# Tree attention on one core: more heads' slots laid side by side by GpSimd, and the first stores cut differently

## The chip, the core and the metric

The kernel runs on one core of one Trainium2 chip. The metric is the device time of one execution in microseconds (us). Three runs of the kernel before gave 133.4, 133.46 and 134.01 us; the median is 133.46 us.

## The reference

Batch 8 times 12 heads are 96 heads of 512 rows and 64 columns. Row `i` may look at itself and at its ancestors in a binary tree, nothing else.

```python
mask[i, i] = 1
parent = i
while parent > 0:
    parent = (parent - 1) // 2
    mask[i, parent] = 1
scores = np.einsum('bhqd,bhkd->bhqk', Q, K) * scale
scores = scores + (1 - mask) * (-1e9)
weights = np.exp(scores - np.max(scores, axis=-1, keepdims=True))
weights = weights / (np.sum(weights, axis=-1, keepdims=True) + 1e-10)
return np.einsum('bhqk,bhkd->bhqd', weights, V).astype(np.float32)
```

## The kernel before

The 96 heads are handled in 48 steps of two heads. The code of a step is written out in a fixed order (`FIRST`, then `SVK` and `SVQ` in turn), and each engine runs its own instructions in that order:

- **S**, scores: TensorE multiplies mask codes (L511, L544) and keys with queries (L519, L554) into PSUM, ScalarE takes the exponential into tiles `e` (L529, L560).
- **V**, values: TensorE multiplies the exponentials with the values `vt` into `ob` (L605); VectorE takes the reciprocal (L651) and writes the product to the output tile `of` (L653).
- **K** and **Q**, turning: from step 8 on, one K turn or one Q turn stands in every step and serves four heads, a few steps before their scores. TensorE transposes K or Q into `ktp` or `qtp`, VectorE copies them into `kq` (L470, L474, L478 for K; L493 for Q).

Heads are loaded in batches of eight (`KB`), so batch 3 is heads 24 to 31. Loads cast from float32 to bf16. In a batch as it is loaded, the two heads that a transpose needs side by side do not lie side by side, and a turn takes 16 transposes that fill 64 output partitions each (L450). For the batches in `LAID`, GpSimd first copies the batch into the tile `besideK` or `besideQ` (function `lay`, L433, two copies, one for each group of four heads), and a turn then takes 8 transposes of 128 output partitions (L441). There is one tile `besideK` and one `besideQ`, so `lay` of a batch also waits until the transposes of the batch before have read it.

The values of 16 heads (an octet of steps, numbered 0 to 5) are loaded into `vst` and spread into the tiles `vt` by GpSimd, VectorE and ScalarE (function `spread`, L364).

GpSimd's work is a list, `pool_program`: loads (`load_k`, `load_q`, `load_rows`, `load_leaves`), spreads, lays and stores (L662) in a fixed order. `ready` decides after which step an entry is written out, never its place in the list. GpSimd runs the list strictly in order; an entry that waits holds back all behind it. Every transfer but the first few and the last goes through this list, and each issue is an instruction of GpSimd. The last four heads are stored by SyncE.

Of the kernel before, what the change touches and what calls it, by code (L numbers as in the profile page):

```python
# [119 lines left out]
def kernel(  # L120
# [7 lines left out]
    nc = tc.nc  # L128
    B, H, S, D = Q.shape
    P = nc.NUM_PARTITIONS  # L130
# [5 lines left out]
    WIDE = 8  # L136
    KB, VB, VO = 8, 16, 16
    EIGHT = 2
    LAID = (8, 9, 10, 11)
    assert NH % VB == 0  # L140

    fp32 = mybir.dt.float32
# [126 lines left out]
    def head(i, a):  # L269

        return 2 * i + a if i < WIDE else 4 * (i // 2) + i % 2 + 2 * a
# [151 lines left out]
    def slots(st, i):  # L423
        return st[2 * i // KB].rearrange("p (g x) t d -> p g (x t) d", x=2)
# [167 lines left out]
    def values(i):  # L592

        if i < NP - 1:
            obs[i] = ob = psO.tile([P, 2, 512], fp32, name="ob")
        else:
            obs[i] = ob = psS.tile([P, 2, 512], fp32, name="s1")
        e1, e2, vt = ets[i], e2s[i % NE], vts[(head(i, 0) // VB) % NV]

        vtile = VTILE if i < WIDE else WVTILE  # L600
        parts = EIGHT_PARTS if head(i, 0) >= VB * EIGHT else PARTS[i >= WIDE]
        assert all(("vt", n, head(i, a)) in issued for n in parts for a in range(2))

        def product(e, a, t, tile_v, lo=0, hi=128, **flags):
            nc.tensor.matmul(  # L605
                out=ob[lo:hi, a, 65 * t:65 * t + 65],
                lhsT=e[:, a, PLACE[t], lo:hi],
                rhs=vt[vtile[tile_v][0]][:, head(i, a) % VB, vtile[tile_v][1], 0:D + 1],
                **flags,
            )  # L610

        def firsts(a):
            for t in range(4):
                product(e1, a, t, 0, start=t == 0, stop=False)

        def halves(a, last=True):
            for t in (0, 1):
                product(e2, a, t, 1 + SELF[t], 0, 64, start=False, stop=last and t == 1)
                product(e2, a, t, 1 + t, 64, 128, start=False, stop=last and t == 1)

        def wholes(a, last=False):
            for t in (2, 3):
                product(e2, a, t, 1 + t, start=False, stop=last and t == 3)

        if i == NP - 1:
            for a in range(2):
                firsts(a)
                wholes(a)
                halves(a)
        elif i >= 4 * LAID[0] - 4:  # L630
            for a in range(2):
                firsts(a)
            for a in range(2):
                halves(a, False)
# [25 lines left out]
    def store(eng, h0, n, step=1, p0=0, p1=P):  # L660
        g, f = divmod(h0, VO)
        return eng.dma_start(  # L662
            out=Or[p0:p1, h0:h0 + step * (n - 1) + 1:step, :],
            in_=ofs[g][p0:p1, f:f + step * (n - 1) + 1:step, :, :].rearrange(
                "p h t d -> p h (t d)"
            ),
        )

    DEALT = (0, 85, 87, 121, P)

    def store_rows(j0, j1):

        for j in range(j0, j1):
            store(nc.gpsimd, 0, 4, 1, DEALT[j], DEALT[j + 1])

    def pool_program():

        ops = [
            (load_k, 2, 2), (load_q, 2, 2), (load_v, 0, 4), (load_v, 4, 4),
            (load_k, 4, 4), (load_q, 4, 4), (load_k, 8, 4),  # L680
            (load_q, 8, 4), (load_v, 8, 8), (load_k, 12, 4),
            (load_q, 12, 4), (load_k, 16, 8), (load_q, 16, 4), (load_rows, 1, "upper"),
            (load_rows, 1, "even"), (load_rows, 1, "odd"), (load_q, 20, 4),
            (load_k, 24, 8), (load_q, 24, 8), (load_rows, 2, "upper"),
            (load_k, 32, 8), (load_leaves, 2, 0), (load_leaves, 2, 1),
            (load_q, 32, 8), (load_rows, 3, "upper"),
            (spread_pool, (1, "Z0", 8, 16), (1, "Z1", 8, 16)),
            (load_k, 40, 8), (load_q, 40, 8), (load_leaves, 3, 0), (load_leaves, 3, 1),
            (spread_top, 2, 0, 16), (spread_pool, (2, "Z0", 0, 16), (2, "Z1", 0, 16)),
            (load_q, 48, 8), (spread_pool, (2, "X", 0, 16)),  # L690
            (load_k, 48, 8), (spread_pool, (2, "N", 0, 16)),
            (load_rows, 4, "upper"), (spread_top, 3, 0, 16),
            (load_k, 56, 8), (load_q, 56, 8), (load_leaves, 4, 0), (load_leaves, 4, 1),
            (spread_pool, (3, "X", 0, 16), (3, "N", 0, 16), (3, "Z0", 0, 16), (3, "Z1", 0, 16)),
            (load_k, 64, 8), (store_rows, 0, 2), (load_q, 64, 8), (store_rows, 2, 4),
            (load_k, 72, 8), (spread_top, 4), (store, nc.gpsimd, 4, 12), (lay, "kst", 8),
            (load_q, 72, 8), (spread_pool, (4, "X", 0, 16), (4, "N", 0, 16)),
            (lay, "qst", 8), (load_rows, 5, "upper"),
            (spread_pool, (4, "Z0", 0, 16), (4, "Z1", 0, 16)),
            (load_leaves, 5, 0), (load_leaves, 5, 1), (load_k, 80, 8), (load_q, 80, 8),  # L700
            (store, nc.gpsimd, 16, 8), (lay, "kst", 9), (load_k, 88, 8), (load_q, 88, 8),
            (lay, "qst", 9), (store, nc.gpsimd, 24, 8), (store, nc.gpsimd, 32, 16),
            (spread_top, 5), (lay, "kst", 10), (store, nc.gpsimd, 48, 16), (lay, "qst", 10),
            (spread_pool, (5, "X", 0, 16), (5, "N", 0, 16)),
            (spread_pool, (5, "Z0", 0, 16), (5, "Z1", 0, 16)),
            (lay, "kst", 11), (store, nc.gpsimd, 64, 8), (lay, "qst", 11),
            (store, nc.gpsimd, 72, 8), (spread_leaves, 5, 1),
            (store, nc.gpsimd, 80, 8), (store, nc.gpsimd, 88, 4),
        ]
        return ops  # L710

    def ready(op, i):

        f, args = op[0], op[1:]
        if f in (load_k, load_q):
            return 2 * (i + 3) >= args[0] + args[1] - 4 * KB
        if f is load_v:
            return True
        if f in (load_rows, load_leaves):
            return 2 * i >= VB * (args[0] - 2)  # L720
        if f is spread_pool:
            tops = [(("vt", "M", VB * o + h) in issued) for o, part, h0, h1 in args if part == "X"
                    and o < EIGHT for h in range(h0, h1)]
            return 2 * i >= VB * (args[0][0] + 1 - NV) and all(tops)
        if f is store_rows:
            return 2 * i >= 4
        if f in (spread_top, spread_leaves):
            return 2 * i >= VB * (args[0] + 1 - NV)
        if f is lay:
            return turned[args[0]] >= 4 * args[1]  # L730
        return 2 * i >= -(-(args[1] + args[2]) // 4) * 4
# [15 lines left out]
    for o in range(EIGHT, NH // VB):  # L747
        for j in range(8):
            h0 = VB // 2 * (j // 4)
# [107 lines left out]
```

## Time and profile before

| what | value |
|---|---|
| median of three runs | 133.46 us |
| the profiled execution | 133.8 us |
| its span, first to last instruction | 131.9 us |
| TensorE matmul busy | 114.7 us (87%) |
| VectorE busy | 108.8 us (82%) |
| ScalarE busy | 94.4 us (72%) |
| GpSimd busy | 87.1 us (66%), 118 instructions |
| granted TensorE clock, mean | 0.978 |

In the profile PE is TensorE, PEld its weight loads, DVE is VectorE, ACT is ScalarE, POOL is GpSimd and SP is SyncE. The page gives a row of digits for each engine: the span in 40 slices of 3.3 us, each digit the busy share of a slice in tenths. A row of the timeline has the start and the length in us, the engine, the line, the operation, out<-in with the shapes, the count, and in brackets the idle time before it with what ended it. A row of the groups has after the first bar the busy time in us and the mean length of one in ns, and after the second bar the idle time before them. The profile counts issuing a transfer as busy time of POOL.

### The profile page before, as it was taken

How to read it: one execution, taken by the hardware profiler on the slowest of the kernel's cores; microseconds unless marked ns; L12 is line 12 of the kernel's file. 1: busy time of each engine (PE TensorE's matmuls, PEld its weight loads, DVE VectorE, ACT ScalarE, POOL GpSimd, SP SyncE). 2: the span in 40 equal slices, each digit the busy share in tenths (PEclk: the TensorE clock that was granted, in tenths of full speed). 3: DMA queues.
4: the chain of work that ended last, by engine and by line, in shares of the span. 5: the costliest groups of instructions: out<-in, count | busy, mean ns of one | idle time of the engine just before them, and what ended most of it. 6: DMA issues, size and time to landing. Idle time of an engine off the chain costs nothing.

```text
span 131.9 us, 5281 instructions
## 1 busy us (share of the span) xinstructions
PE 114.7 (87%) x2286; PEld 80.4 (61%) x2289; DVE 108.8 (82%) x261; ACT 94.4 (72%) x153; POOL 87.1 (66%) x118
## 2 busy tenths in 40 slices
PE   6883999999789699899899999999988999999920
PEld 2351576676566476666577677677765766776610
DVE  3438569988999989989999999999999999877350
ACT  4358268989768957968858787787868668688900
POOL 6994624245623998799951899999999977802200
PEclk9999599999999999999999999999999999999996
DMA  3999999999999999999999999999999999999984
GB/s 122 216 190 196 198 199 205 199 199 207 206 200 205 204 202 208 209 202 205 202 208 204 244 236 305 338 204 207 203 288 285 228 391 406 400 402 402 397 315 148
DMA packets 29719, 32.28 MB, mean 245 GB/s; under 512 B 1488, under 2 KB 26704, under 8 KB 29696
## 3 DMA queue, kind: packets, MB, share of 16 engines
q0 software_dynamic: 28416, 30.68, 115.2%
q1 hardware_dynamic: 864, 0.93, 2.1%
q10 hardware_dynamic: 416, 0.33, 1.0%
q8 instruction: 18, 0.29, 0.8%
q14 instruction: 5, 0.04, 0.1%
HBM read 37.96 MB, written 12.58 MB: 383 GB/s over the span
## 4 chain that ended last, share of the span: by engine, by line
DVE 38%; PE 24%; DMA 14%; POOL 10%; issue 5%; ACT 3%; ACTq 1%; POOLq 0%
DVE of L653 12%; DVE vt L364 11%; DMA kst<-in_K_dram 8%; PE ob L605 8%; DMA qst<-in_Q_dram 6%; POOL vt L364 5%; DVE rec L651 3%; PE s L511 3%; DVE kq L493 3%; DVE kq L470 3%; DVE kq L478 3%; DVE kq L474 3%; PE s L519 2%; ACT e L560 2%; PE s L544 1%
## 5 line engine op out<-in xcount | busy, mean ns | idle before, releaser
L529 ACT ACTIVATE e<-s 128x1024 bf16<-128x1024 f32 x40 | 40.9, 1023 | 20.7 <-PE s L519 20.1
L605 PE MATMUL ob<-vt,e 128*128 128x65 bf16 (+1 forms) x940 | 39.8, 198 | 6.0 <-DVE of L653 3.0
L605 PEld LDWEIGHTS <-e 128*128 128x128 bf16 (+1 forms) x960 | 31.7, 103 | 15.9 <-DVE of L653 5.1
L560 ACT ACTIVATE e<-s 128x384 bf16<-128x384 f32 x80 | 34.7, 491 | 0.0
L653 DVE TENSOR_TENSOR of<-ob,rec 128x512 f32<-128x512 f32 x47 | 32.5, 691 | 1.6
L364 POOL COPY vt<-vst 32x512 int32<-32x512 int32 (+1 forms) x38 | 31.0, 816 | 2.9 <-PE ob L605 1.2
L364 DVE COPY vt<-vst 32x1024 bf16<-32x1024 bf16 (+6 forms) x54 | 26.8, 497 | 2.3 <-DMA vst<-in_V_dram 1.3
L662 POOL DMA_DIRECT2D out_dram<-of x13 | 12.1, 928 | 12.7 <-DVE of L653 9.2
L511 PE MATMUL s<-codes 40*128 40x512 bf16 x96 | 19.3, 398 | 0.7 <-ACT e L525 0.4
L519 PE MATMUL s<-kq 64*128 64x512 bf16 x96 | 18.5, 380 | 0.0
L651 DVE RECIPROCAL rec<-ob 128x8 f32<-128x8 f32 x47 | 9.6, 204 | 8.8 <-PE ob L605 8.0
L554 PEld LDWEIGHTS <-kq 64*128 64x128 bf16 x320 | 12.1, 94 | 4.8
L554 PE MATMUL s<-kq 64*128 64x160 bf16 (+1 forms) x320 | 14.6, 208 | 0.0
L544 PE MATMUL s<-codes 40*128 40x384 bf16 x80 | 13.6, 333 | 0.3
L493 DVE COPY kq<-qtp 128x1024 bf16<-128x1024 bf16 x20 | 13.6, 681 | 0.0
L256 POOL DMA_DIRECT2D qst<-in_Q_dram x11 | 8.3, 752 | 6.8 <-DMA vst<-in_V_dram 2.6
L525 ACT ACTIVATE e<-s 128x1024 bf16<-128x1024 f32 x8 | 8.2, 1022 | 6.0 <-PE s L519 5.9
L544 PEld LDWEIGHTS <-codes 40*128 40x128 bf16 x80 | 6.1, 94 | 7.9 <-issue 1.2
L256 POOL DMA_DIRECT2D kst<-in_K_dram x10 | 7.6, 760 | 3.9 <-PE ob L605 2.8
L470 DVE COPY kq<-ktp 128x256 bf16<-128x256 bf16 x20 | 8.3, 415 | 0.3 <-PE ktp L450 0.3
L474 DVE COPY kq<-ktp 128x256 bf16<-128x256 bf16 x20 | 8.3, 415 | 0.0
L478 DVE COPY kq<-ktp 128x512 bf16<-128x512 bf16 x20 | 8.3, 414 | 0.0
(49 smaller groups left out, 139.4 us busy)
## 6 DMA issues: line engine op xcount, KB each, us to landing
kst<-in_K_dram POOLq DMA_DIRECT2D x10, 512.0 KB, 13.2
out_dram<-of POOLq DMA_DIRECT2D x5, 1024.0 KB, 13.9
qst<-in_Q_dram POOLq DMA_DIRECT2D x9, 512.0 KB, 14.5
out_dram<-of POOLq DMA_DIRECT2D x2, 2048.0 KB, 20.8
vst<-in_V_dram POOLq DMA_DIRECT2D x12, 256.0 KB, 14.9
vst<-in_V_dram POOLq DMA_DIRECT2D x6, 512.0 KB, 14.3
out_dram<-of POOLq DMA_DIRECT2D x1, 1536.0 KB, 10.7
qst<-in_Q_dram POOLq DMA_DIRECT2D x5, 256.0 KB, 11.9
```

The source lines that it names most:

```text
L256: return nc.gpsimd.dma_start(out=kept[b][:, h0 % KB:h0 % KB + n, :, :].rearrange("p (g x) t d -> p g (x t d)", x=2), in_=wide[:, h0 // 2:( ...
L364: return copy(out=dst, in_=src)
L493: nc.vector.tensor_copy(out=qq[:, :, 0:16, :].rearrange("p b u c -> p b (u c)"), in_=halves)
L511: nc.tensor.matmul(out=sp[:, a, :], lhsT=(k1code if i < WIDE else k1wide)[64 * a:64 * a + CODE_ROWS, :], rhs=(q1code[64 * a:64 * a + CODE_ ...
L519: nc.tensor.matmul(out=sp[:, a, :], lhsT=keys(i, a, TOP), rhs=qTs[i][64 * a:64 * a + 64, :, :].rearrange("p t c -> p (t c)"), start=False, ...
L529: ) if i < WIDE else nc.scalar.activation(
L544: nc.tensor.matmul(out=flat[:, a, :, :].rearrange("p u (t c) -> p u t c", t=4)[:, :, :, 16:64], lhsT=k2wide[64 * a:64 * a + CODE_ROWS, :], ...
L554: nc.tensor.matmul(out=flat[:, a, :, lo:hi], lhsT=keys(i, a, WTILE2[t]), rhs=qT[64 * a:64 * a + 64, :, lo:hi], start=False, stop=t == 1, s ...
L560: nc.scalar.activation(out=e2s[i % NE][:, a, :, 32:128].rearrange("p t (r u) -> p t r u", u=2), in_=flat[:, a, :, :].rearrange("p u (t r) ...
L605: nc.tensor.matmul(out=ob[lo:hi, a, 65 * t:65 * t + 65], lhsT=e[:, a, PLACE[t], lo:hi], rhs=vt[vtile[tile_v][0]][:, head(i, a) % VB, vtile ...
L651: nc.vector.reciprocal(out=rec[:, a:a + n, :, :], in_=o4[:, a:a + n, :, D:D + 1])
L653: nc.vector.tensor_tensor(out=ofs[g][:, first:last + 1:step, :, :], in0=o4[:, a:a + n, :, 0:D], in1=rec[:, a:a + n, :, :].to_broadcast([P, ...
```

## The change

`LAID` grows from batches 8 to 11 to batches 3 to 11, so heads 24 to 63 are now laid as well: ten more entries `lay` in GpSimd's list, 20 copies. The order of the value products, which hung on `LAID[0]`, is held at step 28 (`LATE`) as before. The first stores are cut differently. Before, heads 0 to 3 went out in four transfers of 85, 2, 34 and 7 partitions and heads 4 to 15 in one; now heads 0 to 2 go out in 85, 2, 34 and 7 partitions, heads 3 to 5 in 15, 17 and 96, and heads 6 to 15 in one: three transfers more, of the same bytes in all.

```diff
-    LAID = (8, 9, 10, 11)
+    LAID = (3, 4, 5, 6, 7, 8, 9, 10, 11)
+    LATE = 28
...
-        elif i >= 4 * LAID[0] - 4:
+        elif i >= LATE:
...
-    DEALT = (0, 85, 87, 121, P)
+    DEALT = [(h0, p0, p1) for h0, cuts in ((0, (0, 85, 87, 121, P)), (3, (0, 15, 32, P)))
+             for p0, p1 in zip(cuts, cuts[1:])]
 
     def store_rows(j0, j1):
 
-        for j in range(j0, j1):
-            store(nc.gpsimd, 0, 4, 1, DEALT[j], DEALT[j + 1])
+        for h0, p0, p1 in DEALT[j0:j1]:
+            store(nc.gpsimd, h0, 3, 1, p0, p1)
...
-            (load_k, 72, 8), (spread_top, 4), (store, nc.gpsimd, 4, 12), (lay, "kst", 8),
...
+            (lay, "kst", 7), (lay, "qst", 7), (load_k, 72, 8),
+            (store_rows, 4, 6), (spread_top, 4), (store_rows, 6, 7),
+            (store, nc.gpsimd, 6, 10), (lay, "kst", 8),
...
         if f is store_rows:
-            return 2 * i >= 4
+            return 2 * i >= (8 if args[1] > 4 else 4)
```

On GpSimd, from the loads of the leaves of octet 3 to the load of the upper rows of octet 4, stood before (`vt` are spreads, `kst` and `qst` loads):

```order
L294 DMA vst<-in_V_dram 32x8x512 x2
L364 COPY vt_0_107<-vst 32x16x32 x4
L364 COPY vt_1_108<-vst 32x32x32 x2
L256 DMA qst<-in_Q_dram 128x4x512
L364 COPY vt_2_109<-vst 32x32x32
L256 DMA kst<-in_K_dram 128x4x512
L364 COPY vt_2_109<-vst 32x32x32
L285 DMA vst<-in_V_dram 64x16x256
```

There every copy of GpSimd is a spread. At the same place (the line numbers are one higher) now stands:

```order
L295 DMA vst<-in_V_dram 32x8x512 x2
L434 COPY besideK<-kst 128x512 x2
L365 COPY vt_0_107<-vst 32x16x32 x4
L365 COPY vt_1_108<-vst 32x32x32 x2
L257 DMA qst<-in_Q_dram 128x4x512
L434 COPY besideQ<-qst 128x512 x2
L365 COPY vt_2_109<-vst 32x32x32
L257 DMA kst<-in_K_dram 128x4x512
L365 COPY vt_2_109<-vst 32x32x32
L286 DMA vst<-in_V_dram 64x16x256
```

The lays of batch 4, K and Q, have come in between, and everything behind them, loads included, stands behind them on the same engine.

On GpSimd, from the load of Q's batch 8 to the lay of K's batch 8, stood before (`out_dram` are stores, partitions x heads x 256 elements):

```order
L256 DMA qst<-in_Q_dram 128x4x512
L662 DMA out_dram<-of 34x4x256
L662 DMA out_dram<-of 7x4x256
L256 DMA kst<-in_K_dram 128x4x512
L364 COPY vt_0_107<-vst 32x16x32 x4
L662 DMA out_dram<-of 128x12x256
L433 COPY besideK<-kst 128x512 x2
```

Between the same two entries now stands:

```order
L257 DMA qst<-in_Q_dram 128x4x512
L663 DMA out_dram<-of 34x3x256
L663 DMA out_dram<-of 7x3x256
L434 COPY besideK<-kst 128x512 x2
L434 COPY besideQ<-qst 128x512 x2
L257 DMA kst<-in_K_dram 128x4x512
L663 DMA out_dram<-of 15x3x256
L663 DMA out_dram<-of 17x3x256
L365 COPY vt_0_107<-vst 32x16x32 x4
L663 DMA out_dram<-of 96x3x256
L663 DMA out_dram<-of 128x10x256
L434 COPY besideK<-kst 128x512 x2
```

The lays of batch 7 and three more store issues have come in ahead of the lay of K's batch 8. Behind it GpSimd's list is the same as before. VectorE's, ScalarE's and SyncE's instructions stand in the same order as before; TensorE has 160 transposes and 160 weight loads fewer: the 20 turns of heads 24 to 63 take 8 transposes each in place of 16.

More of the change, by code (lines that the diff above doesn't have):

```diff
@@ L686, in pool_program @@
             (load_q, 32, 8), (load_rows, 3, "upper"),
-            (spread_pool, (1, "Z0", 8, 16), (1, "Z1", 8, 16)),
-            (load_k, 40, 8), (load_q, 40, 8), (load_leaves, 3, 0), (load_leaves, 3, 1),
+            (spread_pool, (1, "Z0", 8, 16), (1, "Z1", 8, 16)), (lay, "kst", 3),
+            (load_k, 40, 8), (load_q, 40, 8), (lay, "qst", 3),
+            (load_leaves, 3, 0), (load_leaves, 3, 1), (lay, "kst", 4),
             (spread_top, 2, 0, 16), (spread_pool, (2, "Z0", 0, 16), (2, "Z1", 0, 16)),
-            (load_q, 48, 8), (spread_pool, (2, "X", 0, 16)),
+            (load_q, 48, 8), (lay, "qst", 4), (spread_pool, (2, "X", 0, 16)),
             (load_k, 48, 8), (spread_pool, (2, "N", 0, 16)),
[L692 to L695, printed above, removed]
-            (load_k, 72, 8), (spread_top, 4), (store, nc.gpsimd, 4, 12), (lay, "kst", 8),
+            (load_rows, 4, "upper"), (lay, "kst", 5),
+            (load_k, 56, 8), (load_q, 56, 8), (lay, "qst", 5),
+            (load_leaves, 4, 0), (load_leaves, 4, 1), (spread_top, 3, 0, 16),
+            (spread_pool, (3, "X", 0, 16), (3, "N", 0, 16)), (lay, "qst", 6), (lay, "kst", 6),
+            (load_k, 64, 8), (spread_pool, (3, "Z0", 0, 16), (3, "Z1", 0, 16)),
+            (store_rows, 0, 2), (load_q, 64, 8), (store_rows, 2, 4),
+            (lay, "kst", 7), (lay, "qst", 7), (load_k, 72, 8),
+            (store_rows, 4, 6), (spread_top, 4), (store_rows, 6, 7),
+            (store, nc.gpsimd, 6, 10), (lay, "kst", 8),
             (load_q, 72, 8), (spread_pool, (4, "X", 0, 16), (4, "N", 0, 16)),
```

## The prediction

> **What bounds the kernel now.** I read the page first, for the busy shares and how they lie over the span.
>
> ```profile
> span 131.9 us, 5281 instructions
> PE 114.7 (87%) x2286; PEld 80.4 (61%) x2289; DVE 108.8 (82%) x261; ACT 94.4 (72%) x153; POOL 87.1 (66%) x118
> DVE  3438569988999989989999999999999999877350
> POOL 6994624245623998799951899999999977802200
> DMA  3999999999999999999999999999999999999984
> DVE 38%; PE 24%; DMA 14%; POOL 10%; issue 5%; ACT 3%; ACTq 1%; POOLq 0%
> ```
>
> The mean shares mislead. POOL, at 66%, looks like the engine with room, but its digits show that the room lies ahead of slice 14 (43 us) and in the tail: from 43 to 106 us it is busy but for one dip in slices 21 and 22 (66 to 73 us). VectorE is full from about 30 to 110 us and leads the chain that ended last (38%). The transfers have no free slice either. The windows give each stage in numbers (columns: length, then busy us of PE, PEld, DVE, ACT and POOL with counts, clock, DMA share, GB/s).
>
> ```profile
> 43.00:73.70 30.70, 27.80 (x650) 20.13 (x649) 28.99 (x67) 23.18 (x41) 24.25 (x30) 1.00 1.28 205
> 73.70:93.00 19.30, 18.55 (x401) 13.75 (x394) 18.66 (x43) 15.56 (x27) 18.79 (x26) 1.00 1.22 256
> 84.00:96.00 12.00, 11.84 (x223) 8.69 (x222) 11.60 (x28) 9.34 (x17) 11.87 (x16) 1.00 1.27 218
> ```
>
> From 84 to 96 us TensorE is busy for 11.84 of 12 us, VectorE for 11.60 and GpSimd for 11.87. Three engines are at their limit at once, and whatever delays TensorE or VectorE there by more than 0.2 to 0.4 us is not made up. From 73.7 to 93 us GpSimd has 0.5 us left.
>
> Its timeline from 43 us on names all the idle time that it has (in brackets):
>
> ```profile
> 53.49 2.65 POOL L364 COPY vt<-vst 32x512 int32<-32x512 int32 x4 [1.20 <-PE ob L605]
> ...
> 68.10 1.08 POOL L662 DMA_DIRECT2D out_dram<-of  x1 [1.38 <-DMA kst<-in_K_dram]
> 71.28 0.56 POOL L662 DMA_DIRECT2D out_dram<-of  x1 [2.10 <-DMA qst<-in_Q_dram]
> 72.89 0.78 POOL L256 DMA_DIRECT2D kst<-in_K_dram  x1 [1.04 <-PE ob L605]
> ```
>
> That is 1.20 + 1.38 + 2.10 + 1.04 = 5.7 us up to 72.9 us, and after it none until the lays of batch 9. Each of these waits is for something that happens at its own time (TensorE's products, the landing of an earlier load), so a GpSimd that comes later finds them over: up to 5.7 us of new work costs nothing.
>
> **The change part by part.**
>
> *TensorE's turns.* A turn of 16 half-width transposes against one of 8 whole ones, each with the instruction that follows it:
>
> ```profile
> 70.21 0.61 PE L450 MATMUL ktp<-ptile,kst 128*64 128x128 bf16 x16
> 70.76 0.40 PE L511 MATMUL s<-codes 40*128 40x512 bf16 x2
> ...
> 92.78 0.61 PE L441 MATMUL ktp<-ptile,besideK 128*128 128x128 bf16 x8
> ...
> 94.97 0.61 PE L441 MATMUL qtp<-ptile,besideQ 128*128 128x128 bf16 x8
> 95.51 0.40 PE L511 MATMUL s<-codes 40*128 40x512 bf16 x2
> ```
>
> From the first transpose to the next matmul pass 70.76 - 70.21 = 0.55 us with sixteen and 95.51 - 94.97 = 0.54 us with eight. The halves run in pairs; twenty turns give back 20 x 0.01 = 0.2 us at most. I take nothing.
>
> *GpSimd's lays.* Five batches, K and Q, two copies each: 20 copies. The rows of the copies that are there, with those of the stores and of the spreads:
>
> ```profile
> L364 DVE COPY vt<-vst 32x1024 bf16<-32x1024 bf16 x36 | 19.6, 543 | 1.9 <-DMA vst<-in_V_dram 1.3
> L662 POOL DMA_DIRECT2D out_dram<-of x13 | 12.1, 928 | 12.7 <-DVE of L653 9.2 <-DMA qst<-in_Q_dram 2.1 <-DMA kst<-in_K_dram 1.4
> L364 POOL COPY vt<-vst 32x512 int32<-32x512 int32 (+1 forms) x38 | 31.0, 816 | 2.9 <-PE ob L605 1.2
> L433 POOL COPY besideQ<-qst 128x512 int32<-128x512 int32 x8 | 5.3, 680 | 0.2
> L433 POOL COPY besideK<-kst 128x512 int32<-128x512 int32 x8 | 4.7, 612 | 1.1 <-PE ktp L441 0.9
> ```
>
> One copy takes (5.3 + 4.7) / 16 = 0.625 us, 20 take 12.5 us. Batch 3 is laid ahead of 43 us, where GpSimd is idle more than half of the time (digits 6, 2 and 3 of slices 11 to 13, 33 to 43 us), and its four copies, 2.5 us, are hidden there. Sixteen copies, 10.0 us, fall between 43 us and the lays of batch 8.
>
> *The stores.* Three issues more, all between 70 us and the lay of batch 8. The shortest store issue above took 0.56 us (the one of 7 partitions, at 71.28 us), the mean one 0.928 us; the new ones have 15, 17 and 96 partitions, so I take 0.75 us each, 2.3 us (bounds 1.7 and 2.8). The bytes are the same, so the transfers' own time I take as unchanged.
>
> *The sum on GpSimd.* 10.0 + 2.3 = 12.3 us of new work less 5.7 us of idle time: GpSimd reaches the lay of batch 8 and all behind it 6.6 us later than before. From there on its list is the one of before and has no gap until the lay of batch 11, so it stays 6.6 us late. Whether that costs anything depends on when TensorE wants the laid tiles:
>
> ```profile
> 89.59 1.16 POOL L433 COPY besideK<-kst 128x512 int32<-128x512 int32 x2
> ...
> 92.17 1.39 POOL L433 COPY besideQ<-qst 128x512 int32<-128x512 int32 x2
> ```
>
> The first half of a lay is what the next turn waits for. For K of batch 9 it ends at 89.59 + 0.6 = 90.2 us and TensorE takes it at 92.78 us: 2.6 us of slack, so 6.6 - 2.6 = 4.0 us late. For Q of batch 9 it ends at 92.17 + 0.6 = 92.8 us, wanted at 94.97 us: 2.2 us of slack, 4.4 us late. That is the tightest; what is late by 4.4 us is the turn itself, and TensorE, which runs in order, holds behind it the scores and the values of that step, for which ScalarE and VectorE wait. Since PE and DVE are at 99% and 97% in that window I let at most 0.4 us of it be made up: **4.0 us**. The delays at earlier lays are part of this one and don't add.
>
> *Bounds.* Below: copies at 0.61 us, stores at 0.56 us: 9.8 + 1.7 - 5.7 - 2.2 - 0.4 = 3.2 us. Above: copies at 0.68 us, stores at 0.93 us, and 0.9 us of the idle time left because a landing still comes last: 10.9 + 2.8 - 4.8 - 2.2 = 6.7 us.
>
> *VectorE beside GpSimd.* Two copies of one shape, one while GpSimd works, one while it rests:
>
> ```profile
> 99.84 1.05 DVE L364 COPY vt<-vst 32x1024 bf16<-32x1024 bf16 x1
> ...
> 107.16 0.42 DVE L364 COPY vt<-vst 32x1024 bf16<-32x1024 bf16 x1
> ```
>
> The 36 of that form average 0.543 us, so they lose 36 x (0.543 - 0.42) = 4.4 us to something. If that is GpSimd's copies alone (10.0 us of lays and 31.0 us of spreads), it is 4.4 / 41 = 0.11 us for each us of them, and 12.5 us more cost VectorE 1.3 us. The Trainium skill, in "SBUF — State Buffer", section "SBUF: two separate sides", gives the rule: GpSimd and a two-port VectorE copy take turns on one pair of ports, and the later one waits for the whole instruction of the other. The trace agrees (1.05 against 0.42 us). The rule speaks against this change. I don't add the 1.3 us: VectorE's loss before 93 us moves TensorE's demand for batch 9 later by as much, and GpSimd's lateness covers it.
>
> *The end.* From the turn of Q 9 on nothing is made up (three engines full, then a tail of products), so the last normalisation and the store behind it come 4.0 us later. The last store:
>
> ```profile
> 127.41 0.39 SPq L662 DMA_DIRECT2D out_dram<-of  x1
> ...
> out_dram<-of SPq DMA_DIRECT2D x1, 512.0 KB, 3.6
> ```
>
> Issued at 127.41 us, it lands 3.6 us later, at 131.0 of 131.9 us; it moves with the last step. The profiled execution took 133.8 us with a span of 131.9, and is 0.3 us over the median of 133.46. With 4.0 us more the same execution would take 137.8 us; on the median that is **137.5 us**.
>
> **The rivals.**
>
> *GpSimd stays in time, only the ports cost.* For the lay of Q 9 to be in time, the 12.3 us of new work would have to be at most 5.7 + 2.2 = 7.9 us. Rows for that there are none: it takes copies of 0.35 us. But a position that I have misplaced, or a turn that may come late because its scores are a few steps off, could loosen it. Then VectorE's 1.3 us is what is left: 134.8 us.
>
> *Faster: the transfers are the bound and get better balanced.* The DMA digits are 9 from slice 2 to 38, and in the last stretches
>
> ```profile
> 124.00:128.00 4.00, 2.02 (x46) 1.43 (x40) 2.14 (x7) 1.59 (x3) 0.76 (x1) 1.00 0.91 353
> 128.00:132.00 4.00, 0.00 (x0) 0.00 (x0) 0.00 (x0) 0.00 (x0) 0.00 (x0) 0.68 0.45 162
> ...
> q8 instruction: 18, 0.29, 0.8%
> ```
>
> the queues work to the end. The odd cuts of 85, 2, 34, 7 and now 15, 17, 96 partitions put unequal shares on the 16 DMA engines; if they even out what other work does to them, all transfers end earlier. The mean engine has 0.45 x 4 = 1.8 us of work after 128 us, so an even queue ends near 129.8 in place of 131.0 us: 1.2 us at most, 132.3 us. It decides only if GpSimd is in time (the 7.9 us above), and if the last store's issue, at 127.41 us, is not held up. Against it: the transfers can't end before that store. Queue 8 speaks for it: 0.29 MB in 18 packets are 16 KB each, and 0.8% of 16 engines' 131.9 us over 18 is 0.94 us for one. The Trainium skill ("Runtime: NRT & Kernel Launch", section "Instruction fetch mechanics") has an engine's instructions fetched in blocks of 16 KiB, 256 instructions; by that rule TensorE's 320 instructions fewer save one such packet, and the time would be about 0.9 us less, 132.6 us. The trace shows the packets' size, not whose they are.
>
> *Slower still: the queue runs dry.* Loads behind the new work are issued up to 6.6 us later. If they then land later by all of it, the lay of batch 10 waits for its load as well: 133.46 + 6.6 = 140 us. Against it:
>
> ```profile
> kst<-in_K_dram POOLq DMA_DIRECT2D x10, 512.0 KB, 13.2
> ```
>
> The loads land 13.2 us after their issue in the median, for 512 KB each where the last store's 512 KB took 3.6 us: most of it is time in the queue, and a later issue only shortens it.
>
> **How the numbers follow.** A measurement of this kernel can tell about 0.5% from no change, 0.7 us. GpSimd late at batch 9, 136.7 to 140.2 us by the bounds: 0.70. Only the ports, near 134.8 us: 0.10. The queue runs dry, 140 us: 0.05. The losses and gains cancel, within 0.7 us: 0.05. Faster, 132.3 us: 0.10. So slower 0.85, same 0.05, faster 0.10. The range takes the first two cases: from 134.6 us to 133.46 + 6.7 = 140.2 us; the likeliest case alone runs from 133.46 + 3.2 = 136.7 us.
>
> **What would show it.** Right: in the profile after, POOL without idle time from 43 to past 110 us; turns of batch 9 on TensorE with an idle time that ends with a copy of `besideK` or `besideQ`; that lay some 6 us later than at 89.59 and 92.17 us; VectorE with gaps that end with `ob` after 85 us; the last store some 4 us later. Wrong: TensorE never waits for a `beside` tile. If the time is then 134 to 135 us, the ports alone were it; if it is under 133 us with the last landing close behind the last issue, the transfers were the bound. A turn of eight transposes that is much under 0.54 us would break the first step.

## The result and the profile after

The changed kernel takes 139.56 us (median of six runs, 138.48 to 140.36) against 133.46 us before (six runs, 133.25 to 134.01): a ratio of 1.0444, 95% interval 1.0388 to 1.0499. It is slower by 6.1 us, 2.1 us more than forecast. The profiled execution took 140.1 us. Its page (chain: shares of the span by engine):

```profile
span 138.3 us, 4978 instructions
PE 116.7 (84%) x2126; PEld 82.4 (60%) x2129; DVE 109.4 (79%) x261; ACT 94.4 (68%) x153; POOL 101.4 (73%) x141
POOL 6995343348657999998799999999999999810200
PEclk9999999999999996999999999999999999999975
DMA  4999999999999999999999997999999999999992
GB/s 130 213 193 196 198 202 203 196 205 206 200 206 206 200 208 205 207 203 203 208 200 177 156 168 253 282 166 177 175 192 352 206 327 403 403 402 399 406 396 98
POOL 31%; PE 28%; DVE 19%; DMA 8%; issue 5%; ACT 3%; ACTq 1%; POOLq 0%
```

The transfers' rate on the page of the kernel before:

```profile
GB/s 122 216 190 196 198 199 205 199 199 207 206 200 205 204 202 208 209 202 205 202 208 204 244 236 305 338 204 207 203 288 285 228 391 406 400 402 402 397 315 148
```

VectorE led the chain before with 38%; now GpSimd (POOL) leads it. The row of digits for DMA is almost as full as before, since its digits end at 9, and hides what the row under it shows: in each of the slices 22 to 30 the queues move fewer bytes than in the same slice before. The DMA share of the windows shows it too: 0.99 against 1.22 from 73.7 to 93 us. The windows of the changed kernel (length, busy us of PE, PEld, DVE, ACT, POOL, clock, DMA share, GB/s):

```profile
43.00:73.70 30.70, 27.25 (x492) 19.83 (x490) 26.52 (x59) 21.00 (x37) 28.78 (x40) 0.94 1.28 205
73.70:93.00 19.30, 18.33 (x342) 13.43 (x344) 18.47 (x41) 14.55 (x25) 18.81 (x25) 1.00 0.99 200
93.00:106.50 13.50, 12.15 (x230) 8.81 (x227) 11.96 (x28) 9.49 (x16) 13.23 (x20) 1.00 1.22 222
106.50:127.50 21.00, 20.74 (x392) 15.20 (x390) 17.04 (x41) 17.34 (x30) 14.49 (x19) 1.00 1.07 352
```

and the last two of the kernel before, whose window from 73.7 us stands in the prediction (1.22 and 256 GB/s):

```profile
93.00:106.50 13.50, 12.49 (x231) 8.85 (x228) 13.10 (x30) 9.66 (x18) 13.03 (x16) 1.00 1.19 262
106.50:127.50 21.00, 18.98 (x360) 13.73 (x360) 15.82 (x38) 15.77 (x27) 8.25 (x12) 1.00 1.02 399
```

In the three windows the changed kernel moved 56 x 19.3, 40 x 13.5 and 47 x 21 KB per us less: 1.08 + 0.54 + 0.99 = 2.6 MB. The bytes in all are the same, and at the 400 GB/s of the end 2.6 MB take 6.5 us.

The sizes of the packets in the trace tell what was missing: loads move in packets of 512 and 1024 bytes, GpSimd's stores in packets of 2048 to 4096. From 73.7 to 93 us the stores moved 2.07 MB in both kernels, and the loads 1.72 MB in place of 2.79. So the 1.07 MB that are missing there are loads. They come later and push stores back: from 106.5 to 127.5 us the changed kernel still moves 1.05 MB of loads, where the kernel before moved 0.01. The rate from 73.7 to 93 us in 40 slices of 0.48 us, in the changed kernel and then in the kernel before, shows how they were lost:

```profile
GB/s 207 168 183 127 104 151 146 183 198 199 131 100 100 81 153 217 217 183 193 210 54 160 238 247 380 416 433 399 407 407 295 136 57 81 127 183 191 179 172 177
```

```profile
GB/s 240 268 255 274 262 260 244 237 233 227 204 213 251 257 289 335 363 393 399 399 388 310 327 299 246 242 198 201 194 195 201 195 204 198 201 208 207 199 231 189
```

The rate isn't lower all the time. It drops for half a microsecond to two microseconds, to 104, 81, 54 and 57 GB/s, and returns; before, no slice is under 189.

GpSimd's timeline after, at the lays of batch 9, and TensorE's waits and turns:

```profile
96.86 1.22 POOL L434 COPY besideK<-kst 128x512 int32<-128x512 int32 x2
...
99.51 1.28 POOL L434 COPY besideQ<-qst 128x512 int32<-128x512 int32 x2
```

```profile
PE qtp L442 <- POOL besideQ L434: 4.1, 4, 2.0
...
PE ktp L442 <- POOL besideK L434: 0.9, 1, 0.9
```

```profile
50.55 0.62 PE L442 MATMUL qtp<-ptile,besideQ 128*128 128x128 bf16 x8 [1.97 <-POOL besideQ L434]
...
51.44 0.63 PE L520 MATMUL s<-kq 64*128 64x512 bf16 x2
...
54.98 0.38 PE L520 MATMUL s<-kq 64*128 64x512 bf16 x2
...
97.58 0.62 PE L442 MATMUL ktp<-ptile,besideK 128*128 128x128 bf16 x8 [0.88 <-POOL besideK L434]
...
100.29 0.62 PE L442 MATMUL qtp<-ptile,besideQ 128*128 128x128 bf16 x8 [0.34 <-POOL besideQ L434]
```

The lays are 7.3 us later than at 89.59 and 92.17 us, and TensorE waits for them, which it never did before. The two turns of batch 9 start 4.8 and 5.3 us later than at 92.78 and 94.97 us. But only 0.88 and 0.34 us of that are waits there: TensorE came to the first of them 3.9 us late already. It had waited for lays earlier, for 1.03 us ahead of its turn at 38.91 us (batch 3), for 1.97 at 50.55 (batch 4) and for 0.73 at 89.75 (batch 8).

The last store (timeline, then its row of the issues):

```profile
131.17 0.39 SPq L663 DMA_DIRECT2D out_dram<-of  x1
```

```profile
out_dram<-of SPq DMA_DIRECT2D x1, 512.0 KB, 6.3
```

Its issue, which ends the compute, is 131.17 - 127.41 = 3.76 us later. But it lands 6.3 us after that where it took 3.6, so the landing is 6.4 us later. The profile thus has two late ends: the compute by 3.8 us and the transfers by 6.4 us.

### The profile page after: what moved, and what is told of

It reads as the page before. It is cut to its first block, busy times and chain, and to the rows that moved or that the text cites. A ratio compares the mean times of both kernels' runs of the same rounds, so it can differ in the third digit from the quotient of the medians.

```text
span 138.3 us, 4978 instructions
## 1 busy us (share of the span) xinstructions
PE 116.7 (84%) x2126; PEld 82.4 (60%) x2129; DVE 109.4 (79%) x261; ACT 94.4 (68%) x153; POOL 101.4 (73%) x141
## 4 chain that ended last, share of the span: by engine, by line
POOL 31%; PE 28%; DVE 19%; DMA 8%; issue 5%; ACT 3%; ACTq 1%; POOLq 0%
PE ob L606 9%; DMA kst<-in_K_dram 8%; POOL vt L365 7%; DVE of L654 6%; POOL out_dram L663 5%; DVE vt L365 5%; PE s L512 4%; POOL besideK L434 4%; POOL qst L257 3%; POOL besideQ L434 3%; PE s L520 3%; PE ktp L442 2%; PE qtp L442 2%; PE s L555 2%; PE s L545 2%
## 5 line engine op out<-in xcount | busy, mean ns | idle before, releaser
L530 ACT ACTIVATE e<-s 128x1024 bf16<-128x1024 f32 x40 | 41.0, 1024 | 25.9 <-PE s L520 24.0
L663 POOL DMA_DIRECT2D out_dram<-of x16 | 14.3, 893 | 6.7 <-DVE of L654 6.7
L520 PE MATMUL s<-kq 64*128 64x512 bf16 x96 | 18.5, 382 | 0.0
L442 PE MATMUL qtp<-ptile,besideQ 128*128 128x128 bf16 x144 | 11.1, 220 | 4.1 <-POOL besideQ L434 4.1
L442 PE MATMUL ktp<-ptile,besideK 128*128 128x128 bf16 x144 | 11.4, 224 | 1.2 <-POOL besideK L434 0.9
L434 POOL COPY besideQ<-qst 128x512 int32<-128x512 int32 x18 | 10.9, 634 | 1.2 <-PE qtp L442 1.1
L434 POOL COPY besideK<-kst 128x512 int32<-128x512 int32 x18 | 11.4, 660 | 0.4
L442 PEld LDWEIGHTS <-besideQ 128*128 128x128 bf16 x144 | 8.2, 98 | 4.9 <-POOL besideQ L434 4.5
## 6 DMA issues: line engine op xcount, KB each, us to landing
kst<-in_K_dram POOLq DMA_DIRECT2D x10, 512.0 KB, 12.3
vst<-in_V_dram POOLq DMA_DIRECT2D x6, 512.0 KB, 13.2
```

The lines of the kernel that those rows point to most:

```text
L434: nc.gpsimd.tensor_copy(out=two[:, g, :, :, :].bitcast(int32), in_=src.bitcast(int32))
L442: nc.tensor.transpose(out=out(dst), in_=two[:, 2 * i % KB // 4, s, :, :].rearrange("p a d -> p (a d)"), identity=ptile[:, 0:128],)
L520: nc.tensor.matmul(out=sp[:, a, :], lhsT=keys(i, a, TOP), rhs=qTs[i][64 * a:64 * a + 64, :, :].rearrange("p t c -> p (t c)"), start=False, ...
L530: ) if i < WIDE else nc.scalar.activation(
L663: return eng.dma_start(out=Or[p0:p1, h0:h0 + step * (n - 1) + 1:step, :], in_=ofs[g][p0:p1, f:f + step * (n - 1) + 1:step, :, :].rearrange ...
```

## The experiments

The theories: **A**, GpSimd comes late through the new work, and all that its list issues or lays with it; **B**, the uneven cut loads single DMA engines; **C**, the turns that wait for laid tiles cost the time. The table has the median, the ratio to the kernel before beside it with its 95% interval, GpSimd's lateness at the lay of K's batch 9, and, against before, the issue (compute) and the landing (transfers) of the last store, all three from the profiled execution.

| kernel | us | ratio | lay K 9 | compute | transfers |
|---|---|---|---|---|---|
| changed | 139.56 | 1.044 (1.039 to 1.050) | +7.3 | +3.8 | +6.4 |
| only the new cut | 137.76 | 1.028 (1.024 to 1.032) | +4.4 | +2.3 | +4.7 |
| only the lays | 138.12 | 1.032 (1.027 to 1.037) | +4.7 | +4.1 | +4.6 |
| lays 3 to 7 unused | 139.33 | 1.042 (1.040 to 1.045) | +5.8 | +2.3 | +5.5 |
| none laid | 134.59 | 1.006 (1.004 to 1.009) | none | +1.6 | +0.9 |
| loads ahead | 141.47 | 1.061 (1.055 to 1.067) | +9.7 | +9.7 | +8.9 |
| new cut, same count | 133.68 | 1.002 (1.000 to 1.004) | -0.2 | -0.2 | -0.2 |
| even cut, three more | 135.81 | 1.018 (1.014 to 1.022) | +2.1 | -1.4 | +1.7 |
| before, stores by SyncE | 151.43 | 1.134 (1.131 to 1.137) | +5.8 | +18.3 | +17.6 |
| batch 7 too | 134.62 | 1.008 (1.005 to 1.011) | +1.4 | -1.2 | +0.3 |
| one store, three fewer | 134.17 | 1.004 (1.002 to 1.006) | -0.7 | -1.6 | +0.9 |
| changed, 2 MB less stored | 135.55 | 1.014 (1.011 to 1.018) | +5.8 | +2.3 | +1.5 |
| before, 2 MB less stored | 131.85 | 0.987 (0.984 to 0.990) | +0.4 | -1.4 | -2.1 |

The last three columns are of one execution each, and executions of one program differ there by up to 1.5 us. The changed kernel with 2 MB less stored is the same program until GpSimd comes to the store left out, behind the lay of K's batch 10, and yet its lay of K's batch 9 comes 1.5 us earlier than in the changed kernel. The kernel before with 2 MB less stored is the kernel before up to the same place, and its turn that stands at 49.01 us comes 1.0 us earlier.

**Each half alone.** The kernel before with the new `DEALT` and its list entries, and the changed kernel with the old ones:

```diff
-            (load_k, 72, 8), (spread_top, 4), (store, nc.gpsimd, 4, 12), (lay, "kst", 8),
+            (load_k, 72, 8), (store_rows, 4, 6), (spread_top, 4), (store_rows, 6, 7),
+            (store, nc.gpsimd, 6, 10), (lay, "kst", 8),
```

> The kernel before with the new cut of the first stores alone and no further lays. Theory A (GpSimd's lateness is the cause, and it leaves the transfer queue short of work): three more issues, about 2.3 us, fall into GpSimd's 5.7 us of idle time, so within 0.7 us of 133.5 us. Theory B (the uneven cut loads single DMA engines and costs the transfers): most of the loss, 137 us or more. Theory C (the turns waiting for laid tiles are all of it): as before, 133.5 us.

> The changed kernel with the old cut of the first stores: heads 0 to 3 in 85, 2, 34 and 7 partitions and heads 4 to 15 in one transfer. Theory A: GpSimd late by some 5 us in place of 7.3 us, so 136.5 to 138.5 us. Theory B: near 134.5 us. Theory C: as the changed kernel, 139.5 us.

Each half alone costs over 4 us, and the two together only 6.1. For the lays A's number held. For the cut it missed: three issues in GpSimd's idle time should have cost nothing. GpSimd's timeline in the kernel with only the cut shows why:

```profile
72.73 0.78 POOL L256 DMA_DIRECT2D kst<-in_K_dram  x1 [0.80 <-PE s L519]
73.72 0.59 POOL L662 DMA_DIRECT2D out_dram<-of  x1 [0.20 <-issue]
76.22 1.06 POOL L662 DMA_DIRECT2D out_dram<-of  x1 [1.92 <-PE ob L605]
...
79.96 1.79 POOL L662 DMA_DIRECT2D out_dram<-of  x2
81.79 1.36 POOL L433 COPY besideK<-kst 128x512 int32<-128x512 int32 x2
```

The three issues more take 0.59 + 1.06 + about 0.8 us, close to my 2.3, but there is a new wait of 1.92 us too. The view names TensorE's products, which were long done for heads 3 to 5. By the program, an issue of GpSimd waits for the landing of the transfer eight issues back; for this one that is the load of K's batch 8, which the trace has landing at 75.93 us, 0.3 us ahead. So eight of its transfers may be under way, and in no trace here are there more, however small, and pieces of 6 to 102 KB take up places. The idle times before two earlier pieces (1.38 and 2.10 us in the kernel before) are the same kind of wait and stay too.

**Are laid tiles worth anything?** First the lays are made but the turns of batches 3 to 7 read the loaded tiles (16 half transposes again); then the kernel before with no batch laid.

```diff
-        two = laid.get((name, 2 * i // KB))
+        two = laid.get((name, 2 * i // KB)) if 2 * i // KB >= 8 else None
```

> The changed kernel with the lays of batches 3 to 7 still made, but TensorE turning these batches from the loaded tiles with 16 half transposes. Only the use of these lays is left out. Theory A: GpSimd is as late as ever for batches 8 and 9 and for its loads, so 138.5 to 140 us. Theory C (waits of TensorE for the new lays): these waits are gone and the time falls to 135 us or less.

> The kernel before with no batch laid at all: 16 copies fewer on GpSimd, every turn with 16 half transposes. If a turn costs TensorE 0.55 us in either form, as the profile before shows, and GpSimd's copies only stretch VectorE's: 132.3 to 133.5 us, with the transfers, which have no gap, as the floor. If the whole-width turn is worth something (fewer instructions to fetch, or a faster TensorE in the last 20 us, where it is the bound): slower, 134 us or more.

C falls as the cause of the time, as far as the new lays go: with nobody waiting for lays 3 to 7, 139.33 us. (The turns of batches 8 and 9 still wait in this kernel, for 1.33, 0.87 and 0.33 us.) The compute is late by 2.3 us without those waits and by 3.8 with them, but the transfers, late by 5.5 us, cover the difference. With none laid, the time is 0.6% longer. TensorE's timeline without lays

```profile
91.15 0.89 PE L605 MATMUL ob<-vt,e 128*128 128x65 bf16 x20
91.97 0.64 PE L450 MATMUL ktp<-ptile,kst 128*64 128x128 bf16 x16
92.55 0.40 PE L511 MATMUL s<-codes 40*128 40x512 bf16 x2
...
93.47 0.89 PE L605 MATMUL ob<-vt,e 128*128 128x65 bf16 x20
```

and before

```profile
92.05 0.89 PE L605 MATMUL ob<-vt,e 128*128 128x65 bf16 x20 [0.16 <-DVE of L653]
...
94.24 0.90 PE L605 MATMUL ob<-vt,e 128*128 128x65 bf16 x20
```

gives 2.32 us for a step against 2.19. The laid turn saves 0.13 us there: 0.03 to 0.04 in the turn and 0.09 ahead of it (products to turn 91.97 - 91.15 = 0.82 us, and 92.78 - 92.05 = 0.73 before). On the mean nothing is left of it, since VectorE holds up some of the shorter steps: the 14 steps from 87.43 to 120.14 us take 2.34 us each before, and the 10 from 86.53 to 109.76 us without lays 2.32. What the kernel without lays loses, it loses later. TensorE stands idle twice, in the midst of a turn and of a step's products:

```profile
112.23 0.33 PE L450 MATMUL ktp<-ptile,kst 128*64 128x128 bf16 x5 [1.12 <-issue]
...
119.80 0.52 PE L605 MATMUL ob<-vt,e 128*64 128x65 bf16 x11 [1.19 <-issue]
```

"Issue" is time in which the engine waits for nothing that the profile shows. What these 2.3 us are stays open.

**Order, count or evenness.** Four kernels, each with one edit: the loads of batches 8 and 9 and of octet 5 ahead of lays and spreads in the changed kernel; the same number of issues as before with a cut of heads 0 to 2; heads 4 to 15 in four even transfers; and the stores from head 16 on SyncE.

```diff
-            store(nc.gpsimd, 0, 4, 1, DEALT[j], DEALT[j + 1])
+            store(nc.gpsimd, 0, 3, 1, DEALT[j], DEALT[j + 1])
...
-            (load_k, 72, 8), (spread_top, 4), (store, nc.gpsimd, 4, 12), (lay, "kst", 8),
+            (load_k, 72, 8), (spread_top, 4), (store, nc.gpsimd, 3, 13), (lay, "kst", 8),
```

> The kernel before with heads 0 to 2 (not 0 to 3) in 85, 2, 34 and 7 rows, and heads 3 to 15 in one transfer: as many store issues as before, almost the same cut. Theory A (what counts is GpSimd's issues): 133.5 us, within 0.7. Theory B (how the cut spreads bytes on the 16 DMA engines is finely tuned, and the other number of heads spoils it): over 134.5 us.

```diff
+    DEALT += [(4, 12, p0, p0 + 32) for p0 in (0, 32, 64, 96)]
...
-            (load_k, 72, 8), (spread_top, 4), (store, nc.gpsimd, 4, 12), (lay, "kst", 8),
+            (load_k, 72, 8), (spread_top, 4), (store_rows, 4, 8), (lay, "kst", 8),
```

> The kernel before with the store of heads 4 to 15 issued as four transfers of 32 rows each, where it was one: three issues more, in an even cut, with nothing else changed. Theory A (three issues more at GpSimd, and with them the wait for the transfer eight issues back, make all loads behind them late): 137 to 138 us, as the kernel with only the new cut (137.8). Theory B (the uneven pieces of 15, 17 and 96 rows load single DMA engines): 133.5 to 134.5 us, since 32 rows are even.

B falls as the main cause: almost the old cut with the old count is no slower, and an even cut with three issues more costs 1.8%. Whether the uneven pieces cost something beside it is not shown: three uneven pieces more take 137.76 us and three even ones 135.81, but with the uneven ones GpSimd is 2.3 us later as well, and no run has them without that. A's size for the even cut was too large (135.81, not 137 to 138): its four issues took 2.47 us together without the wait of 1.92. This run separates the two ends. GpSimd is 2.1 us late at batch 9, the turns wait for it for 0.62 and 0.34 us and start within 0.4 us of before, and the compute ends no later than before (1.4 us earlier, of which this execution leads by 1.0 us at 51 us already, ahead of its edit), yet the time is 2.3 us longer. The first of these turns in TensorE's timeline, then the last store in SyncE's timeline and in the issues:

```profile
92.41 0.62 PE L441 MATMUL ktp<-ptile,besideK 128*128 128x128 bf16 x8 [0.62 <-POOL besideK L433]
```

```profile
125.99 0.39 SPq L662 DMA_DIRECT2D out_dram<-of  x1
```

```profile
out_dram<-of SPq DMA_DIRECT2D x1, 512.0 KB, 6.8
```

```diff
-            (load_k, 64, 8), (spread_pool, (3, "Z0", 0, 16), (3, "Z1", 0, 16)),
-            (store_rows, 0, 2), (load_q, 64, 8), (store_rows, 2, 4),
-            (lay, "kst", 7), (lay, "qst", 7), (load_k, 72, 8),
...
+            (spread_pool, (3, "N", 0, 16)), (load_q, 64, 8), (lay, "qst", 6), (lay, "kst", 6),
+            (store_rows, 0, 2), (spread_pool, (3, "Z0", 0, 16), (3, "Z1", 0, 16)),
+            (store_rows, 2, 4), (load_k, 72, 8), (store_rows, 4, 7),
+            (store, nc.gpsimd, 6, 10), (lay, "kst", 7), (load_q, 72, 8), (lay, "qst", 7),
```

> The changed kernel with the same work on GpSimd in another order: around batches 6 to 8 the loads of K 64, Q 64, K 72 and Q 72 and of the V rows of octet 5 stand ahead of the lays and most spreads, so that they are issued some 2 to 4 us earlier; what GpSimd does in all is the same, and the lays of batches 8 and 9 come no earlier. Theory A in the form that the loads' lateness counts (the transfer queue short of work from 73 to 106 us): it recovers 1 to 2.5 us, 137 to 138.5 us. Theory A in the form that only the lays' lateness counts: 139 to 140 us, no change from the changed kernel. Theory B (uneven cut): no change either.

Both forms of A missed: 141.47 us. The page's rate of the transfers and GpSimd's timeline show what the new order did:

```profile
GB/s 135 212 191 195 197 202 202 197 206 204 201 206 206 201 208 206 206 201 206 206 206 231 234 387 165 177 22 59 161 161 342 219 310 402 401 401 406 399 328 157
```

```profile
83.75 0.84 POOL L286 DMA_DIRECT2D vst<-in_V_dram  x1
...
95.72 1.15 POOL L295 DMA_DIRECT2D vst<-in_V_dram  x2
```

The loads put ahead had landed, lays and spreads then filled 11 us without one issue, and the queue ran dry (22 and 59 GB/s, 91 to 98 us). It only moved the hole and made it deeper.

```diff
-            (store, nc.gpsimd, 16, 8), (lay, "kst", 9), (load_k, 88, 8), (load_q, 88, 8),
+            (store, nc.sync, 16, 8), (lay, "kst", 9), (load_k, 88, 8), (load_q, 88, 8),
...
```

> The kernel before with the stores of heads 16 to 91 issued by SyncE, which has nothing else to do there, in place of GpSimd: GpSimd loses seven issues of 0.93 us, all after 85 us, and the loads and lays behind them come earlier. Theory A (GpSimd's list sets when the transfers start, and in the kernel before the lays of batch 9 still have 2 us of slack): 132 to 133.5 us, little gain, since TensorE and VectorE are full there too. Theory that the end is the transfers': no change, 133.5 us, or up to 1 us slower if stores now overtake loads in the queue.

Missed by 18 us. I had taken it that the stores would leave at their old place, after 85 us. SyncE has nothing to wait for but the normalised heads; its timeline and the chain's first part of the page:

```profile
45.07 9.28 SPq L662 DMA_DIRECT2D out_dram<-of  x2
```

```profile
DMA 49%; PE 20%; DVE 12%; POOL 10%; issue 3%; ACT 2%; ACTq 1%; POOLq 0%
DMA qst<-in_Q_dram 27%; DMA kst<-in_K_dram 22%; PE ob L605 6%; DVE vt L364 4%; DVE of L653 4%; PE s L511 3%; POOL vt L364 2%; PE s L519 2%; PE qtp L441 2%; POOL vst L244 2%; POOL kst L244 2%; POOL qst L244 1%; PE s L554 1%; PE ktp L450 1%; PE s L544 1%
```

Two megabytes went out from 45 us on, beside loads that TensorE soon waits for, and the loads of K and Q became half of the chain. GpSimd's long list had kept stores behind loads. The Trainium skill ("DMA: Bandwidth & Descriptors", section "Queues, rings and completion order") has a DMA engine take the rings that have work in turn; the run agrees in that with stores in a second queue the loads of K took 18.5 us to land in the median, where they took 13.2.

**Less to move, one batch, fewer issues.** The store of heads 48 to 63 taken out of both kernels; batch 7 alone laid in addition to the old four; and heads 0 to 3 in one transfer.

```diff
-            (lay, "qst", 9), (store, nc.gpsimd, 24, 8), (store, nc.gpsimd, 32, 16),
-            (spread_top, 5), (lay, "kst", 10), (store, nc.gpsimd, 48, 16), (lay, "qst", 10),
+            (lay, "qst", 9), (store, nc.gpsimd, 24, 8), (store, nc.gpsimd, 32, 16),
+            (spread_top, 5), (lay, "kst", 10), (lay, "qst", 10),
```

> The changed kernel without the store of heads 48 to 63 (2 MB that are not written; all else is computed). In the changed kernel the last store is issued 3.8 us later than before and lands 6.3 us after that, where it took 3.6. Theory Q (the last 2.5 us are transfers that pile up because too few bytes moved from 73 to 106 us): 2 MB less at 400 GB/s are 5 us of transfers, the pile is gone, the last store lands 2.5 to 3.6 us after its issue, which stays at 130 to 131.5 us: 136 to 137.3 us. Theory A alone (only TensorE's late turns count and the landing is one of the chip's own): 139 to 140 us, unchanged.

> The control: the kernel before without the store of heads 48 to 63 (2 MB that are not written). If its end is set by the compute, as the 3.6 us of its last store say, it takes 132.3 to 133.5 us, 0 to 1.2 us less than before. If the transfers set the end there too, it falls by 2.5 us or more, under 131 us.

In the changed kernel (its row of the issues)

```profile
out_dram<-of SPq DMA_DIRECT2D x1, 512.0 KB, 2.8
```

the pile is gone, as Q expects, and the time falls by 4.0 us; Q's range missed by 0.5 us. The control falls by 1.7 us, half a microsecond more than a bound by compute alone would give and less than one by the transfers alone; its last store lands after 2.9 us. In both profiled executions the compute ends 1.4 us earlier than with all stores, but they lead by as much by 54 us, ahead of the store left out, so it belongs to the execution and not to the edit. The medians don't hang on it: with less to move the changed kernel is 135.55 - 131.85 = 3.7 us slower, as much as its compute is late, and with all to move 6.1. The other 2.4 us are transfers.

```diff
-    LAID = (8, 9, 10, 11)
+    LAID, LATE = (7, 8, 9, 10, 11), 28
...
+            (lay, "kst", 7), (lay, "qst", 7), (load_k, 72, 8),
```

> The kernel before with one batch more laid, batch 7 (four copies, 2.5 us, at the place where GpSimd had 4.5 us of idle time from 66.7 to 72.9 us). If idle time at GpSimd takes up new work, as the prediction had it: 133 to 134 us, the lays of batch 9 less than 1 us later than before. If new work there pushes the issues behind it, as the three stores did: the lays of batch 9 some 2.5 us later, which TensorE's slack of 2.2 to 2.6 us still covers, and 133.5 to 135.5 us by the loads' lateness.

```diff
-            store(nc.gpsimd, 0, 4, 1, DEALT[j], DEALT[j + 1])
+            store(nc.gpsimd, 0, 4)
...
-            (load_k, 64, 8), (store_rows, 0, 2), (load_q, 64, 8), (store_rows, 2, 4),
+            (load_k, 64, 8), (store_rows, 0, 1), (load_q, 64, 8),
```

> The kernel before with heads 0 to 3 stored in one DMA at the place of the first of its four pieces: three issues fewer on GpSimd (0.56 to 1.08 us each, and the waits of 1.38 and 2.10 us before two of them). If issues and the waits for the transfer eight issues back are what makes GpSimd late, it is up to 2.5 us earlier at the lays of batch 9, more bytes are queued at a time, and the time is 132 to 133.5 us. If the loads then only wait elsewhere, 133.5 us, no change.

Of 2.5 us of new copies 1.1 were taken up by idle time, by these two executions: GpSimd is 1.4 us late. No turn waits for it, and the compute ends no later, but the median is 1.1 us up. The profiled execution, 0.65 us under its median, shows 0.3 us of it at the landing; where the rest lies stays open. Three issues fewer give nothing: a wait of 4.78 us for TensorE takes their place.

```profile
71.50 2.69 POOL L364 COPY vt<-vst 32x512 int32<-32x512 int32 x4 [4.78 <-PE ob L605]
```

No version that computes everything beat the kernel before.

**What feeds the queue.** From each transfer's issue and landing in the trace follows how many KB were under way at a time, on the mean from 73.7 to 93 us; beside it the rate from the same window:

```text
kernel                  KB under way   GB/s
none laid                   3292       256
one store, three fewer      3175       259
before                      2826       256
batch 7 too                 2304       250
even cut, three more        2138       233
only the lays               1686       225
loads ahead                 1568       224
only the new cut            1547       228
lays 3 to 7 unused          1481       211
changed                     1328       200
```

The kernels with 2.3 MB or more under way moved 250 GB/s and more, those with less 200 to 233. The order is not strict, and it does not show that the one makes the other, since both fall when fewer bytes are issued. Nor need few bytes under way slow the queue: at 82.4 us the changed kernel had three transfers under way, 608 KB, where the kernel before had three of 2560 KB, and from 81 to 83 us it still moved 204 GB/s, nearly all loads, as in the window from 43 us (205). What the traces show are stretches in which the DMA engines are less busy: in the changed kernel their share is 0.66 from 75 to 76 us, 0.90 from 79 to 81, 0.56 from 83 to 84 and 0.72 from 89 to 90, against 1.04 to 1.40 in the same stretches before, and the loads move after them. Lays hold GpSimd from issuing, and small pieces take up places among eight. Which share each has in these stretches, and whether small pieces also hold up single DMA engines there, is not shown.

## Why the prediction was right and wrong

The forecast of 137.5 us, 4.0 more, stood on GpSimd coming late and TensorE waiting for it; the result, 139.56, is inside the range, with a second cause that I had priced at 0.05. That it is inside is in part luck: the upper bound of 140.2 came from longer copies and issues, and what filled it were transfers.

- *TensorE's turn gains nothing*: true for the time, not for the turn. I read from the first transpose to the next matmul (0.55 against 0.54) and left out the 0.09 us ahead of it. That makes 0.13 us in a step that nothing holds up, and nothing on the mean of the steps (2.34 us with lays, 2.32 without).
- *Lays at 0.625 us*: right. After, (11.4 + 10.9) / 36 = 0.62 us in the groups:

```profile
L434 POOL COPY besideK<-kst 128x512 int32<-128x512 int32 x18 | 11.4, 660 | 0.4
L434 POOL COPY besideQ<-qst 128x512 int32<-128x512 int32 x18 | 10.9, 634 | 1.2 <-PE qtp L442 1.1
```

- *Stores at 0.75 us each, 2.3 in all*: the issues are right (about 2.45); the wait of 1.92 us that they bring was missing.
- *5.7 us of idle time take up new work*: right in the sum, since GpSimd was 7.3 us late where I had 6.6 (5.8 in the execution with less stored), and wrong as a rule. The cut alone found none of it (4.4 us late), batch 7 alone 1.1 of 2.5 us. The two longest of these idle times (1.38 and 2.10 us) are waits for landings, and landings move when issues do.
- *Slack of 2.2 to 2.6 us at batch 9, compute +4.0*: the number is right, +3.76, and the path only in part, so that it is this close is luck. I had TensorE in time up to batch 9 and held there for 4.0 us. It came there 3.9 us late and was held for 0.88 and 0.34 us more. Its lateness had grown at the lays of batches 3, 4 and 8 (waits of 1.03, 1.97 and 0.73 us), which I had as hidden or as parts of the same delay; without the waits for lays 3 to 7 the compute is 2.3 us late, not 3.8. After the turn of Q 9, which was 5.3 us late, 1.6 us were made up, where I allowed 0.4. Other kernels say the same of the rule: by lateness less 2.2 us of slack the one with only the lays should end its compute 2.5 us late and did 4.1, though no turn of batch 9 waits in it, and the one with lays 3 to 7 unused 3.6 and did 2.3.
- *The transfers' own time unchanged, the last store lands after 3.6 us*: the step that failed. It took 6.3 us; the runs with less stored price it at 2.4 us. I had set the rival of the dry queue aside because loads took 13.2 us to land, most of it waiting in the queue. The median of K's loads did fall only to 12.3 us. But it says nothing of the time between them: four times from 73.7 to 93 us the DMA engines were less busy, the rate there fell by a fifth, 1.07 MB of loads moved later, and the stores that they pushed back had to move at the end.
- *Ports, 1.3 us on VectorE*: not seen in the sum, 541 ns for the copies after against 543:

```profile
L365 DVE COPY vt<-vst 32x1024 bf16<-32x1024 bf16 x36 | 19.5, 541 | 1.2 <-DMA vst<-in_V_dram 0.6
```

In the kernel with the even cut, which has not one copy of GpSimd less, the same 36 took 479 ns each. So my price for each us of GpSimd's copies was wrong. That it hangs on which copies meet would fit, and no run shows it.
- *The rival of fewer instruction packets, 0.9 us faster*: the packets went from 18 to 16 with 160 matmuls and 160 weight loads fewer, and stayed 18 with the new cut alone. The Trainium skill ("Runtime: NRT & Kernel Launch", section "Instruction fetch mechanics") has blocks of 256 instructions, by which 320 fewer save one or two packets; the count agrees. No gain in time is seen: with lays 3 to 7 unused there are 18 packets again, and the time is 139.33 us against 139.56 with 16.

## What to carry to other kernels

Ask of an engine that issues the transfers not only when what it computes is wanted, but how many bytes are under way while it computes: two ends run side by side here, and work that is hidden from one (the turns, with 2 us of slack) is paid at the other (the transfers' end). Idle time that is a wait for a landing is no free room, since new work or small transfers in front of it move the landing. A full row of DMA digits doesn't say that the queues are full: the digits end at 9, and the DMA share (0.99 against 1.22) and the rate showed the hole. Compare rates for the same mix of transfers, since the kernel before moved 205 GB/s where there were loads alone (from 43 to 73.7 us) and 399 where there were stores alone (from 106.5 to 127.5 us).

## What the runs showed of the hardware

TensorE's clock fell to half for 3.41 us after a wait of 1.97 us (granted-clock records of the changed kernel, from 51.2 us), and after a wait of 2.03 us in the kernel with only the new cut (from 87.35 us); the scores' matmuls at 51.44 us took 0.63 us against 0.38 at 54.98. Where the longest wait for a lay was 1.3 us (only the lays, lays unused), the clock stayed whole in all windows from 43 us on. The Trainium skill ("TensorE: Matmul & The Clock Gate", section "Part 1: The HAM clock gate") has the half clock come after at least one idle window of about 3.4 us. The length agrees with such a window; the waits ahead of it were shorter than one. Nor is it the length of one wait alone: in the kernel before two waits of 0.87 and 0.97 us, ahead of the turns at 11.47 and 12.85 us, were followed by 3.41 us at half clock as well (from 13.41 us). The prediction did not have this cost. In the changed kernel TensorE's turns went from 1.5 us late, at 50.55 us, to 2.8 while the clock was half; by 84 us the kernel with only the lays, without a half clock there, was as late (3.2 us against 2.9), so at the end nothing of it is seen.
